# Dividing the opening feed-forward group of a streaming encoder layer like the two that follow it

## The chip, the cores and the metric

The kernel runs on one core of a Trainium2 chip. A core has a matrix engine (PE, whose weight loads are listed as PEld), a vector engine (DVE), a scalar engine (ACT), a small general engine (POOL) and a sequencer (SP) that issues nearly all transfers between the large memory (HBM) and the on-chip memory. Each engine works through its own list of instructions in order, and waits on semaphores for the others. The metric is the device time of one execution in microseconds (us), the median of several runs.

## The reference

One layer, with a prompt of 2048 tokens and 64 decode tokens, model width 1024, feed-forward width 2816. It is an attention-like half (a combined input projection, a pooling mixer and an mLSTM, an output projection) and a feed-forward half. The change touches the second half only in what it computes how, and the first in what is done beside it. The feed-forward half is:

```python
h2 = rmsnorm(x, g2) * (1 + sc2) + sh2
up = h2 @ w_up                                   # 1024 -> 2 x 2816
upp = jnp.concatenate([conv_buf.astype(up.dtype), up], 1)
conv = b_conv + sum(w_conv[j] * upp[:, j:j + T] for j in range(CONV_W))
a, g = jnp.split(conv, 2, -1)
x = x + gt2 * ((jax.nn.silu(g) * a) @ w_down)    # 2816 -> 1024
```

All of it is in 32-bit floating point.

## The kernel before, in words

**Numbers.** A 32-bit matrix is split by ACT into a rounded high part (line 411 for weights) and by DVE into the rest (line 414), and each product is three matmuls (high by high, high by low, low by high; `PASSES`). A weight unit is 128 x 512 of a matrix. SP loads it, ACT and DVE split it, and PE then uses it.

**The attention half** (0 to about 793 us) works through four groups of 512 tokens, the last with the 64 decode tokens added. In each group come the projections for v and the gates (line 1117), twelve projections for the four heads (line 477, with the mLSTM's small matmuls between them), four for the pooling mixer, and the eight rows of the output projection (line 477 too, from `mx`). In this half a scheduler orders the instructions of each engine.

**The feed-forward half** works through three groups of 704 tokens. In each group the 2816 features are 22 blocks of 128. The up projection of a block (line 1572) uses Strassen's scheme with seven products of 352 columns, 84 matmuls a block. Its weight sums (`wsum`) were worked out earlier, beside the attention half, by a generator called `up_sums`. In the list of weights each block has seven units; in the opening group all seven are split by ACT and DVE, and three of them are then stored in split form (`wsplit`, line 419), so that in the later groups only four are split and three are loaded ready.

The down projection comes after each part of the 22 blocks. `PARTS` says how they are divided. A plain part multiplies its blocks by 8 rows of output in two pieces of 448 and 256 columns (line 2138), 48 matmuls a block. A part of four blocks (`paired`) in the second and third group instead goes through `quad_down`, Strassen's scheme over two by two blocks of output rows, features and tokens (line 2015): 168 matmuls of 352 columns for four blocks. Its weight sums (`dsum`) come from `w_quad` and are worked out by the generator `quad_sums` in the opening group. For Strassen's scheme the gated activations are also added and subtracted on DVE before they are split (lines 1775, 1779, 1791).

**Order.** Here in the second half every engine but SP keeps the order in which the code is written. Generators of side work stand in lists `bg[0]` to `bg[4]`, and `tick(i)` runs the first of a list up to its next `yield`. `up_sums` stands in `bg[4]`, ticked four times in each projection of the attention half from the second group on, but not in the pooling projections, nor in the first two output rows. What is left of the lists is run at once in `leave`, after the first two output rows of the last group (`drain(1, 2, 3, 4)`). `leave` then closes the memory of the attention half and opens that of the feed-forward half (`f1`), and starts `norm_sums`, which loads the normed activations (`fscr` from `h2d`, line 802) and makes their sums and splits for the first up projection (`hx`, lines 764, 768 and 782). A side list `prepare` does the same for the next group while the current one runs.

Of the kernel before, what the change touches and what calls it, by code (L numbers as in the profile page):

```python
# [9 lines left out]
F32 = mybir.dt.float32  # L10
F32R = mybir.dt.float32r
AF = mybir.ActivationFunctionType
ALU = mybir.AluOpType
# [19 lines left out]
PARTS = (((0, 5), (5, 10), (10, 16), (16, 22)),) + (((0, 4), (4, 8), (8, 12), (12, 16), (16, 22)),) * 2  # L33
NQ = 4


def paired(g, part):
    return g > 0 and part[1] - part[0] == NQ
# [26 lines left out]
def tile_layer(ctx: ExitStack, tc: tile.TileContext, xT, vecs, cst, rst, w_mod, w_ada, w_qkou, w_v, w_pool,  # L65
# [276 lines left out]
    for g in range(NFG):  # L342
        held = None
        late = []
        for (f0, f1_) in PARTS[g]:
# [7 lines left out]
            if paired(g, (f0, f1_)):  # L353
                held = f0 // NQ
                continue
# [481 lines left out]
    if True:  # L837
# [6 lines left out]
        def up_sums():  # L844

            def load(f, c):
                w = a1.tile([P, 4, 256], F32, tag="w4", name="w4", bufs=4)
                for i in range(2):
# [3 lines left out]
            todo = [(f, c) for f in range(NF) for c in (0, 256)]  # L852
# [4 lines left out]
            for i, (f, c) in enumerate(todo):  # L857
                w = nx.pop(0)
                yield
# [12 lines left out]
                pin(nc.sync.dma_start(out=wsum[f, :, :, c:c + 256], in_=w))  # L872
# [748 lines left out]
    def quad_sums():  # L1621

        for d in range(8):
            for c in (0, 256):
                t = f2.tile([P, 2, FT], F32R, tag="av", name="qs", bufs=AVB)
                w = t.bitcast(F32).rearrange("p a t -> p (a t)")[:, :1024].rearrange("p (i c) -> p i c", i=4)
                nc.sync.dma_start(out=w, in_=w_quad[d, :, :, c:c + 256])
                for _ in range(5):
                    yield
                a11, a12, a21, a22 = (w[:, i] for i in range(4))  # L1630
                dve.tensor_tensor(out=a22, in0=a21, in1=a22, op=ALU.add)
                yield
                dve.tensor_tensor(out=a21, in0=a11, in1=a21, op=ALU.subtract)
                yield
                dve.tensor_tensor(out=a11, in0=a22, in1=a11, op=ALU.subtract)
                yield
                dve.tensor_tensor(out=a12, in0=a12, in1=a11, op=ALU.subtract)
                yield
                yield
                nc.sync.dma_start(out=dsum[d, :, :, c:c + 256], in_=w)  # L1640
                yield
                yield
                yield

# [647 lines left out]
```

## Time and profile before

| What | Value |
|---|---|
| Median of 3 runs | 2180.22 us (2180.21 to 2184.07) |
| Span of the profiled execution | 2178.0 us |
| PE, DVE, ACT busy | 2155.1, 1631.7, 1093.7 us |
| Opening feed-forward group, second, third | 468.2, 452.1, 464.2 us |
| Transfers | 539.51 MB, 248 GB/s over the span |

The groups' times are from the start of one group's first up projection to the next one's; the third ends with the span. A row of the timeline gives the start, the length, the engine, the line, the operands (out<-in) and how many instructions are merged. Lengths of matmuls overlap, so a pace is worked out from starts. In a table of windows each engine has its busy time and, in brackets, its instructions; the last two columns are the share of time that the 16 DMA engines were busy, and what they moved.

### The profile page before, as it was taken

The numbers are of one execution on the slowest core, as the hardware profiler recorded it, in microseconds if no ns is written. First come the engines' busy times: TensorE is split into PE (matmuls) and PEld (weight loads), VectorE is DVE, ScalarE is ACT, GpSimd is POOL, SyncE is SP. The second block draws the span as 40 slices with busy tenths as digits, with TensorE's granted clock in tenths as the row PEclk, the third lists the DMA queues.
The fourth block names the chain that finished last, engine by engine and source line by source line (L and its number), as shares of the span: only waits on it lengthen the run. The fifth ranks groups of instructions, "written<-read, shape, count | busy, mean of one in ns | idle before, by whom it ended". The sixth has DMA issues, their size and how long they took to land.

```text
span 2178.0 us, 38112 instructions
## 1 busy us (share of the span) xinstructions
PE 2155.1 (99%) x13553; PEld 2041.6 (94%) x13553; DVE 1631.7 (75%) x3040; ACT 1093.7 (50%) x2181; POOL 241.6 (11%) x474
## 2 busy tenths in 40 slices
PE   8999999999999999999999999999999999999998
PEld 7888888888899999999999999999999999999998
DVE  5868668757955678797967668888886587887874
ACT  4554335234333456474736445655655364565554
POOL 0010000001000101010101121100101331111112
PEclk9999999999999999999999999999999999999999
DMA  8886997988879387788967966666668675555542
GB/s 325 327 297 226 312 312 259 310 291 273 296 263 305 130 279 255 267 306 295 349 211 257 316 244 225 237 201 215 227 220 275 217 255 183 170 179 190 172 161 81
DMA packets 297351, 539.51 MB, mean 248 GB/s; under 512 B 25760, under 2 KB 114336, under 8 KB 297160
## 3 DMA queue, kind: packets, MB, share of 16 engines
q1 hardware_dynamic: 287720, 514.75, 69.8%
q10 hardware_dynamic: 9440, 22.32, 2.6%
q8 instruction: 107, 1.75, 0.3%
q14 instruction: 84, 0.69, 0.1%
HBM read 410.98 MB, written 125.98 MB: 247 GB/s over the span
## 4 chain that ended last, share of the span: by engine, by line
PE 82%; DMA 7%; DVE 7%; issue 2%; ACT 1%; SPq 1%; POOL 0%; DVEq 0%; POOLq 0%; ACTq 0%
PE mm L1572 35%; PE mm L477 19%; PE mm L2138 12%; PE mm L2015 8%; PE mm L1117 2%; DVE wt L414 2%; DMA raw<-w_ada 1%; DMA wt<-wsum 1%; DMA hl_kept<-wt 1%; DMA wsum<-w 1%; PE m L1307 1%; PE m L1329 1%; PE m L1327 1%; PE m L1292 1%; DVE scr L250 1%
## 5 line engine op out<-in xcount | busy, mean ns | idle before, releaser
L1572 PE MATMUL mm<-hx,wt 128*128 128x352 f32 x5544 | 887.0, 321 | 3.7 <-DVE hx L768 1.9
L1572 PEld LDWEIGHTS mm<-hx,wt 128*128 128x128 f32 x5544 | 878.6, 188 | 6.8 <-DVE hx L768 2.8
L477 PE MATMUL mm<-hl,wt 128*128 128x512 f32 (+2 forms) x1920 | 386.2, 357 | 0.2 <-ACT va L250 0.2
L411 ACT ACTIVATE wt<-raw 128x512 fp32r<-128x512 f32 (+3 forms) x470 | 276.8, 597 | 185.2 <-PE mm L477 63.5
L477 PEld LDWEIGHTS mm<-hl,wt 128*128 128x128 f32 x1920 | 315.4, 189 | 48.2 <-issue 5.3
L414 DVE TENSOR_TENSOR wt<-raw,wt 128x512 fp32r<-128x512 f32 (+3 forms) x470 | 312.2, 670 | 53.2 <-ACT wt L411 52.7
L2138 PE MATMUL mm<-av,wt 128*128 128x448 f32 (+1 forms) x1632 | 262.7, 322 | 0.0
L2138 PEld LDWEIGHTS mm<-av,wt 128*128 128x128 f32 x1632 | 250.4, 188 | 11.1
L1987 DVE SCALAR_TENSOR_TENSOR x<-mm,MOD,x 128x352 f32<-128x352 f32 (+3 forms) x360 | 167.2, 503 | 79.2 <-PE mm L2138 65.7
L2015 PE MATMUL mm<-av,wt 128*128 128x352 f32 x1344 | 220.6, 323 | 1.8 <-DVE x L1987 0.7
L2015 PEld LDWEIGHTS mm<-av,wt 128*128 128x128 f32 x1344 | 215.4, 188 | 4.8 <-DVE ea L1581 2.8
L1619 ACT ACTIVATE mm<-mm 128x352 f32<-128x352 f32 x196 | 87.8, 448 | 240.0 <-PE mm L1572 184.0
L477 PE MATMUL mm<-mx,wt 128*128 128x512 f32 (+1 forms) x960 | 182.6, 352 | 0.0
L477 PEld LDWEIGHTS mm<-mx,wt 128*128 128x128 f32 x960 | 159.3, 188 | 22.5
L1550 DVE SCALAR_TENSOR_TENSOR ta<-ea,V,ta 128x704 f32<-128x704 f32 (+1 forms) x132 | 125.6, 952 | 63.2 <-ACT ta L1545 51.2
L1550 DVE SCALAR_TENSOR_TENSOR tg<-eg,V,tg 128x704 f32<-128x704 f32 (+1 forms) x132 | 125.7, 952 | 61.0 <-ACT tg L1545 58.5
L414 DVE TENSOR_TENSOR wt<-wt 128x512 fp32r<-128x512 f32 x196 | 132.7, 683 | 12.8 <-ACT wt L411 12.7
L411 ACT ACTIVATE wt<-wt 128x512 fp32r<-128x512 f32 x196 | 119.2, 622 | 43.1 <-DMA wt<-wsum 40.1
L1759 ACT ACTIVATE tg<-tg 128x704 f32<-128x704 f32 (+1 forms) x66 | 52.5, 795 | 70.5 <-DVE tg L1550 70.5
L1528 POOL COPY ea<-UC 128x2 f32<-128x2 f32 x66 | 32.8, 497 | 482.6 <-DVE ta L1550 394.0
L1117 PE MATMUL mm<-wt,hl 128*128 128x256 f32 (+1 forms) x576 | 71.3, 284 | 0.0
L1117 PEld LDWEIGHTS mm<-wt,hl 128*128 128x128 f32 x576 | 70.4, 190 | 0.8 <-issue 0.6
(304 smaller groups left out, 2188.2 us busy)
## 6 DMA issues: line engine op xcount, KB each, us to landing
wt<-wsplit SPq DMA_DIRECT2D x132, 512.0 KB, 4.2
raw<-w_up SPq DMA_DIRECT2D x198, 256.0 KB, 3.8
wt<-hl_kept SPq DMA_DIRECT2D x96, 512.0 KB, 6.0
wt<-wsum SPq DMA_DIRECT2D x132, 256.0 KB, 5.3
wsplit<-wt SPq DMA_DIRECT2D x66, 512.0 KB, 5.5
w<-w_up SPq DMA_DIRECT2D x88, 256.0 KB, 3.7
wsum<-w SPq DMA_DIRECT2D x44, 512.0 KB, 4.9
Bd<-fscr ACTq DMA_DIRECT2D x56, 352.0 KB, 4.3
```

The costliest lines, as they stand in the source:

```text
L411: act.activation(u.w[:, 0, :u.n], u.raw[:, :u.n], AF.Copy)
L414: dve.tensor_tensor(out=u.w[:, 1, :u.n], in0=u.raw[:, :u.n], in1=u.w[:, 0, :u.n].bitcast(F32), op=ALU.subtract)
L477: pe.matmul(ps[bi][:, :hi - lo], U[:, a, k % 4 * P:(k % 4 + 1) * P], mv[k][:, b, lo:hi], start=(at == 0 and pi == 0), stop=(k == order[-1] ...
L1117: pe.matmul(ps[ti][:n, :cols], h[4 * kh + k4][:, b, lo:lo + n], U[:, a, k4 % 2 * cols:(k4 % 2 + 1) * cols], start=(kh == 0 and k4 == 0 and ...
L1528: pool.tensor_copy(ext[:, 0:2], UC[:, f, :])
L1550: dve.scalar_tensor_tensor(out=t[:, :E], in0=ext[:, j:j + E], scalar=wc(j, f), in1=t[:, :E], op0=ALU.mult, op1=ALU.add)
L1572: pe.matmul(bk.t[:, :FH], U[:, a, kc * P:(kc + 1) * P], Bo.at(nm, kc, b), start=(first and kc == 0 and pi == 0), stop=(kc == 3 and pi == 2 ...
L1619: act.activation(to.t[:, :FH], bk.t[:, :FH], AF.Copy)
L1759: act.activation(self.tg[:, :E], self.tg[:, :E], AF.Silu)
L1987: dve.scalar_tensor_tensor(out=x3[n][:, a:b], in0=bk.t[:, a - lo:b - lo], scalar=gt2(n, s), in1=x3[n][:, a:b], op0=ALU.mult, op1=ALU.add)
L2015: pe.matmul(bk.t[:, :FH], U[:, a, c:c + P], quad.put(op, m, b), start=(first and m == 0 and pi == 0), stop=(m == 1 and pi == 2), skip_grou ...
L2138: pe.matmul(bks[i].t[:, :hi - lo], U[:, a, k % 4 * P:(k % 4 + 1) * P], av[k][:, b, lo:hi], start=(k == 0 and (a, b) == PASSES[0]), stop=(k ...
```

## The change

All three groups use the same `PARTS`, and `paired` no longer asks for the group. So in the opening group sixteen of the 22 blocks go through `quad_down` in four parts of four, and the last six stay plain. The sums `dsum` are needed earlier: `quad_sums` goes, and its sixteen pieces are appended to the list of `up_sums`, behind the 44 pieces of `wsum`. A piece then takes three ticks where it took four.

```diff
-PARTS = (((0, 5), (5, 10), (10, 16), (16, 22)),) + (((0, 4), (4, 8), (8, 12), (12, 16), (16, 22)),) * 2
+PARTS = ((0, 4), (4, 8), (8, 12), (12, 16), (16, 22))
 NQ = 4
-def paired(g, part):
-    return g > 0 and part[1] - part[0] == NQ
+def paired(part):
+    return part[1] - part[0] == NQ
...
             def load(f, c):
                 w = a1.tile([P, 4, 256], F32, tag="w4", name="w4", bufs=4)
+                if f >= NF:
+                    tc.keep_in_program_order(nc.sync.dma_start(out=w, in_=w_quad[f - NF, :, :, c:c + 256]))
+                    return w
                 for i in range(2):
...
-            todo = [(f, c) for f in range(NF) for c in (0, 256)]
+            todo = [(f, c) for f in range(NF + 8) for c in (0, 256)]
...
             for i, (f, c) in enumerate(todo):
                 w = nx.pop(0)
-                yield
                 yield
...
-                pin(nc.sync.dma_start(out=wsum[f, :, :, c:c + 256], in_=w))
+                pin(nc.sync.dma_start(out=(wsum[f] if f < NF else dsum[f - NF])[:, :, c:c + 256], in_=w))
...
-    def quad_sums():
-        for d in range(8):
-            for c in (0, 256):
-                t = f2.tile([P, 2, FT], F32R, tag="av", name="qs", bufs=AVB)
-                w = t.bitcast(F32).rearrange("p a t -> p (a t)")[:, :1024].rearrange("p (i c) -> p i c", i=4)
-                nc.sync.dma_start(out=w, in_=w_quad[d, :, :, c:c + 256])
...
-        for pi, part in enumerate(PARTS[o.g]):
+        for pi, part in enumerate(PARTS):
...
-            quad = Quad() if paired(o.g, part) else None
+            quad = Quad() if paired(part) else None
...
-                    if o.g == 0:
-                        bg[0].append(quad_sums())
                     bg[1].append(prepare(fgroups[o.g + 1], fscr))
```

The line numbers of the changed file differ: 1574 there is 1572 before, 1993 is 2015, 2114 is 2138; 865, 866, 868 and 869 are 863, 864, 866 and 867, and 874 is 872.

**PE, opening feed-forward group.** Before, the first plain part comes behind the fifth block's products:

```order
L1572 MATMUL mm<-hx,wt 128x352 x330
L2138 MATMUL mm<-av,wt 128x448 x3
L2138 MATMUL mm<-av,wt 128x256 x3
...
L1572 MATMUL mm<-hx,wt 128x352 x12
L2138 MATMUL mm<-av,wt 128x448 x9
L2138 MATMUL mm<-av,wt 128x256 x9
```

and with the change:

```order
L1574 MATMUL mm<-hx,wt 128x352 x330
L719 MATMUL m_9599<-fscr,ones_r 128x352
L720 MATMUL m_9599<-fscr,ones_r 128x352
L719 MATMUL m_9603<-fscr,ones_r 128x352
L720 MATMUL m_9603<-fscr,ones_r 128x352
L1993 MATMUL mm<-av,wt 128x352 x24
L1574 MATMUL mm<-hx,wt 128x352 x12
L1993 MATMUL mm<-av,wt 128x352 x144
L1574 MATMUL mm<-hx,wt 128x352 x324
```

Four such passes of 168 stand where three plain parts of five, five and six blocks stood; PE's order ahead of this place is the same but for one matmul. In all 768 plain matmuls go and 672 of 352 columns come.

**DVE, first output rows of the last attention group** (`w` is the tile of a piece of sums, the rows of line 250 end an output row, line 768 is the first split of `norm_sums`). Before:

```order
L250 SCALAR_TENSOR_TENSOR scr<-mm,MOD,scr 128x64
L863 TENSOR_TENSOR w_7516<-w_7516 128x256
L414 TENSOR_TENSOR wt<-raw,wt 128x512
L864 TENSOR_TENSOR w_7516<-w_7516 128x256
L866 TENSOR_TENSOR w_7516<-w_7516 128x256
L867 TENSOR_TENSOR w_7516<-w_7516 128x256
L414 TENSOR_TENSOR wt<-raw,wt 128x512
L250 SCALAR_TENSOR_TENSOR scr<-mm,MOD,scr 128x256 x2
```

With the change:

```order
L250 SCALAR_TENSOR_TENSOR scr<-mm,MOD,scr 128x64
L865 TENSOR_TENSOR w_7627<-w_7627 128x256
L414 TENSOR_TENSOR wt<-raw,wt 128x512
...
L869 TENSOR_TENSOR w_7627<-w_7627 128x256
L865 TENSOR_TENSOR w_7687<-w_7687 128x256
...
L869 TENSOR_TENSOR w_7687<-w_7687 128x256
L865 TENSOR_TENSOR w_8264<-w_8264 128x256
L866 TENSOR_TENSOR w_8264<-w_8264 128x256
L250 SCALAR_TENSOR_TENSOR scr<-mm,MOD,scr 128x256 x2
L250 SCALAR_TENSOR_TENSOR scr<-mm,MOD,scr 128x64
L868 TENSOR_TENSOR w_8264<-w_8264 128x256
L414 TENSOR_TENSOR wt<-raw,wt 128x512
L869 TENSOR_TENSOR w_8264<-w_8264 128x256
```

Three pieces stand there in place of one, and the last of them ends behind the next output row's addition.

**SP, the same place.** Before:

```order
L640 DMA x2d<-scr 128x576
L872 DMA wsum<-w_7382 512x1x256
L872 DMA wsum<-w_7516 512x1x256
L594 DMA scr<-xT 128x576
L390 DMA raw<-wo_in 128x512
L390 DMA raw<-w_up 128x512
L802 DMA fscr<-h2d 128x704 x4
```

With the change:

```order
L874 DMA dsum<-w_7627 512x1x256
L390 DMA raw<-w_up 128x512
L874 DMA dsum<-w_7687 512x1x256
L640 DMA x2d<-scr 128x576
L390 DMA raw<-w_up 128x512
L874 DMA dsum<-w_8264 512x1x256
L594 DMA scr<-xT 128x576
L390 DMA raw<-w_up 128x512
L802 DMA fscr<-h2d 128x704 x4
```

The first load of `norm_sums` (line 802) stands behind the last store of a piece in both, and its memory is that of the pieces; there are three stores ahead of it now and there were two.

More of the change, by code (lines that the diff above doesn't have):

```diff
@@ L344, in tile_layer @@
         late = []
-        for (f0, f1_) in PARTS[g]:
+        for (f0, f1_) in PARTS:
             for f in range(f0, f1_):
@@ L352, in tile_layer @@
                     held, late = None, []
-            if paired(g, (f0, f1_)):
+            if paired((f0, f1_)):
                 held = f0 // NQ
```

18 lines of the change are left out of this document (1 added, 17 removed).

## The prediction

> **What bounds the kernel now.** I read the page's shares first, then its chain of waits by engine.
>
> ```profile
> span 2178.0 us, 38112 instructions
> PE 2155.1 (99%) x13553; PEld 2041.6 (94%) x13553; DVE 1631.7 (75%) x3040; ACT 1093.7 (50%) x2181; POOL 241.6 (11%) x474
> PE 82%; DMA 7%; DVE 7%; issue 2%; ACT 1%; SPq 1%; POOL 0%; DVEq 0%; POOLq 0%; ACTq 0%
> ```
>
> PE is busy in 99% of the span, so a matmul removed is worth its pace, as long as PE is fed. Then the table of windows, cut where the first up projection of the opening and of the next group starts, and PE's waits in the opening group (first three rows) and in the next (last two).
>
> ```profile
> 793.50:1261.70 468.20, 465.29 (x2922) 456.26 (x2921) 358.63 (x593) 258.17 (x468) 47.21 (x95) 1.00 0.81 278
> 1261.70:1713.80 452.10, 450.89 (x2831) 446.63 (x2830) 359.80 (x580) 256.25 (x473) 52.65 (x97) 1.00 0.68 232
> ...
> PE mm L1572 <- DVE hx L768: 1.9, 3, 0.8
> PE mm L1572 <- DVE wt L414: 0.8, 1, 0.8
> PE mm L1572 <- DVE eg L1581: 0.2, 1, 0.2
> ...
> PE mm L2015 <- DVE x L1987: 0.7, 1, 0.7
> PE mm L2015 <- DVE wt L414: 0.4, 1, 0.4
> ```
>
> The columns are PE, PEld, DVE, ACT, POOL, the granted clock, the DMA share and GB/s. The second group already does what the change makes of the opening one: it is 16.1 us shorter. Of this 2.9 - 1.1 = 1.8 us are waits, so 14.3 us is the work. This is the model for the sum, but the opening group has three things the second lacks: its start hangs on sums made just before, it splits seven weight units a block and not four, and its `dsum` must come from the attention half.
>
> **Term 1, the matmuls: -13.8 us.** The pace is read from starts in PE's timeline, the last plain part of the opening group first, then one Strassen pass of the second.
>
> ```profile
> 1213.92 4.04 PE L2138 MATMUL mm<-av,wt 128*128 128x448 f32 x24
> 1217.79 2.06 PE L1572 MATMUL mm<-hx,wt 128*128 128x352 f32 x12
> 1219.69 42.15 PE L2138 MATMUL mm<-av,wt 128*128 128x448 f32 x264
> 1261.68 0.64 PE L1572 MATMUL mm<-hx,wt 128*128 128x352 f32 x3
> ...
> 1409.41 4.19 PE L2015 MATMUL mm<-av,wt 128*128 128x352 f32 x24
> 1413.44 2.06 PE L1572 MATMUL mm<-hx,wt 128*128 128x352 f32 x12
> 1415.34 23.23 PE L2015 MATMUL mm<-av,wt 128*128 128x352 f32 x144
> 1438.41 51.65 PE L1572 MATMUL mm<-hx,wt 128*128 128x352 f32 x324
> ```
>
> Six plain blocks take (1217.79 - 1213.92) + (1261.68 - 1219.69) = 45.9 us for 288 matmuls, 0.159 us each. A pass takes (1413.44 - 1409.41) + (1438.41 - 1415.34) = 27.1 us for 168, 0.161 each. All 22 blocks plain are 1056 x 0.1592 = 168.1 us; four passes and six plain blocks are 4 x 27.1 + 45.9 = 154.3 us. The difference is 13.8 us, 0.5 below the 14.3 of the two groups.
>
> **Term 2, the start of the half: +4.0 us.** The chain of waits around 758 us, with DVE's and SP's timeline there, shows what the opening group's start hangs on.
>
> ```profile
> 758.43 5.40 DMA wsum<-w
> 763.91 3.18 DMA fscr<-h2d
> 802.08 7.24 PE mm L1572 x44
> ...
> 756.13 0.41 DVE L863 TENSOR_TENSOR w<-w 128x256 f32<-128x256 f32 x1
> 757.98 0.42 DVE L867 TENSOR_TENSOR w<-w 128x256 f32<-128x256 f32 x1
> 759.15 0.69 DVE L414 TENSOR_TENSOR wt<-raw,wt 128x512 fp32r<-128x512 f32 x1 [0.75 <-ACT wt L411]
> 761.54 1.07 DVE L250 SCALAR_TENSOR_TENSOR scr<-mm,MOD,scr 128x256 f32<-128x256 f32 x3 [1.70 <-PE mm L477]
> ```
>
> The last store of a piece goes out at 758.43, lands 5.4 us later, and only then may the first load of `norm_sums` go (763.91), since it overwrites the pieces' memory; from there the chain runs through `hx` to PE at 802, where PE loses the 1.9 us above. With the change three pieces stand where one stood. The first ends at 758.4 as now; the second's four instructions (0.42 each) with a split between them (about 0.6) end at 760.7; half of the third follows, then the output row's addition, which PE releases at 761.54, then the other half with a split: 764.0. The last store moves by 764.0 - 758.4 = 5.6 us, and so does the first load. About 1.7 us of DVE's other work there (one more addition of an output row and one of a sum of squares stand ahead of the first `hx` split in the new order) is done meanwhile and no longer in the way. I take 4.0; the bounds are 0, if the chain behind has slack that its rows do not show, and 5.6.
>
> **Term 3, DVE in the four passes: +2.2 us.** One pass with the blocks behind it is 80.4 us in the second group. The last two rows are DVE's densest stretches in the opening group now; below them is one block's splits back to back.
>
> ```profile
> 1329.00:1409.40 80.40, 80.34 (x505) 80.05 (x505) 69.20 (x116) 49.50 (x93) 6.48 (x16) 1.00 0.64 218
> ...
> 955.20:968.10 12.90, 12.90 (x83) 12.90 (x82) 12.79 (x23) 9.57 (x18) 1.66 (x4) 1.00 0.97 357
> 1060.50:1075.00 14.50, 13.74 (x85) 13.39 (x85) 13.49 (x23) 10.86 (x20) 1.55 (x4) 1.00 1.02 371
> ...
> 1070.20 1.28 DVE L414 TENSOR_TENSOR wt<-wt 128x512 fp32r<-128x512 f32 x2
> ```
>
> DVE has 69.2 us of work in 80.4 us. In the opening group three more units a block are split, 12 in such a stretch; two take 1.28 us, so 12 take 7.7 us, and DVE has 76.9 us, 96%. `quad_sums` is gone from there, which the 69.2 never held. The two dense rows say what 96% costs: at 12.79 of 12.90 us PE lost nothing, at 13.49 of 14.50 it lost 0.76, the one wait of 0.8 above. I take one such loss in each of the four stretches, 3.2 us, less the 1.0 us of waits on `L414` and `L1581` that go with the old parts: 2.2. The bounds are 0.1 (the 1.1 us of the second group) and 6.6: if DVE is never busier than 13.49 of 14.50 (93%), a stretch takes 76.9 / 0.93 = 82.7, 2.3 more, 9.2 in four, with a part of the 1.0 and of the last stretch, which holds less of `prepare`, off. ACT, at 49 of 80 us in the second group, is far from this.
>
> **Term 4, the pieces in the attention half: +1.5 us.** Sixteen pieces more are 64 DVE instructions and 32 transfers of 0.5 MB. They do not spread: a piece now takes three ticks, so the three projection stretches hold 16 pieces each and not 12.
>
> ```profile
> 236.00:340.00 104.00, 103.83 (x559) 86.15 (x559) 69.90 (x161) 35.27 (x106) 7.73 (x9) 1.00 0.91 302
> 410.00:514.00 104.00, 104.00 (x587) 87.38 (x580) 68.31 (x157) 35.59 (x101) 6.08 (x8) 1.00 0.88 290
> 600.00:706.00 106.00, 104.97 (x780) 99.41 (x780) 60.40 (x164) 40.65 (x126) 6.50 (x9) 1.00 0.86 284
> ...
> SPq L849 <- DMA wsum<-w: 97.1, 36, 5.9
> SPq L395 <- PE mm L477: 22.3, 22, 3.5
> SPq L395 <- PE mm L1117: 13.0, 8, 2.7
> ```
>
> DVE has room (70 of 104 us, and four pieces are 4 x 4 x 0.42 = 6.7 us). The transfers hardly have: the first stretch moves 31.4 MB at a share of 0.91, so 332 GB/s would be full; with 4 x 1.05 MB more it needs 35.6 / 332 = 107.2 us of its 104. The others come to 104.2 of 104 and 104 of 106. What hides this is the lead of the weight loads: SP waited 35.3 us for PE to free a buffer (the L395 rows), and at shares of 0.97 and 1.02 (the dense rows) PE lost no more than the 0.76 above. The bounds are 0 and the 3.4 us of overflow; I take 1.5, nearer to the dense rows. The Trainium skill, DMA: Bandwidth & Descriptors, Specifications, gives about 358 GB/s from HBM for a core, by which 35.6 MB would need 99.4 us (an estimate) and this term would be 0; in this trace the dense rows reach 371, so that figure is no firm limit here, and 332 is that stretch's own.
>
> **The sum** is made against the profiled execution: 2178.0 - 13.8 + 4.0 + 2.2 + 1.5 = 2171.9 us of span. The median of the runs is 2.2 us above this span, so 2174.1, and I predict 2174 us, 0.28% less. The work of `quad_sums` leaves the opening group for nothing: it stood on DVE and on the queue, not on PE.
>
> **The rivals.** (A) *SP is blocked by the pieces, and the change is slower.* In row L849 a load of a piece waits 36 times, 97.1 us in all, 2.7 each, for an earlier piece's store to land, and everything behind it on SP waits too, the attention half's weights above all. Sixteen pieces more, closer together, add 16 x 2.7 = 43 us. Against it speaks that the 97 us cost PE nothing, and the 35.3 us of SP's own lead. But that lead is spread over the half, and the waits fall into the projection stretches; if half of it counts there, 43 - 18 = 25 us come to PE: 2174.1 - 1.5 + 25 = 2198 us. It makes the change slower from 12 us on.
>
> (B) *DVE sets the pace of the passes*, at the upper bound of term 3: 2174.1 + 4.4 = 2178.5. For it speaks 96%, and that work waits in order behind additions that PE releases; against it, 12.79 of 12.90 without a loss.
>
> (C) *The losses are hidden*: terms 2 and 4 are near 0 and 3 near its lower bound: 2178.0 - 13.8 + 0.1 + 2.2 = 2166.5. For it speaks that the second group lost 1.1 us only; against it, that the store is on the chain of waits.
>
> **How the numbers follow.** The sum as worked out has a chance of 0.60, A 0.12, B 0.15, C 0.13. About 0.2% (4.4 us) is what a measurement of this kernel can tell from no change, so faster is below 2175.9 and slower above 2184.6. The forecast's own range, 2169 to 2179, from terms 2 to 4 partly at their bounds, lies with 0.46 below 2175.9, 0.13 within and 0.01 above. C is faster; B is 0.02 faster, 0.11 the same, 0.02 slower; A is 0.02 the same, 0.10 slower. In all: faster 0.61, the same 0.26, slower 0.13. From 2166 to 2183 the range holds C's time, the forecast and B; A is left out above and a little below.
>
> **What would show it.** Term 1: line 1993 with 2016 matmuls, and four passes of some 27 us in the opening group. Term 2: the first load of line 802 about 5 us later against the end of the attention half, and PE's wait for `hx` at 6 us and not 1.9. Term 3: PE's waits for DVE in the passes of the opening group near 3 us, with DVE over 90% there. Term 4: PE's waits and starts between 214 and 742 us as before, with the DMA share near 1 in the three stretches. The prediction is wrong if the attention half ends more than 5 us later (A), or if the stretches of the opening group are longer than 83 us (B).

## The result and the profile after

The changed kernel takes 2202.95 us (median of 4 runs, 2200.3 to 2205.5) against 2182.07 us for the kernel before in the same comparison: ratio 1.0096, 95% interval 1.0084 to 1.0109. It is 21 us slower, where 2174, 6 us below the 2180.22 of the kernel before, had been forecast; 2203 lies far outside 2166 to 2183. Times are medians of the executions in the fast state; one execution of the kernel with the pieces only, 2790 us at a granted clock of 0.713, is left out.

The page's span, its engines and the chain of waits by engine, after:

```profile
span 2203.7 us, 38114 instructions
...
PE 2152.6 (98%) x13457; PEld 2037.3 (92%) x13457; DVE 1685.8 (76%) x3152; ACT 1126.8 (51%) x2245; POOL 255.6 (12%) x474
...
PE 77%; DMA 9%; DVE 9%; issue 2%; ACT 2%; SPq 1%; POOL 0%; DVEq 0%; ACTq 0%; POOLq 0%
```

PE's busy time fell by only 2.5 us, its share of the chain from 82% to 77%; transfers and DVE took up what PE lost. The table of windows says in which stage (columns as in the prediction): the attention half from 214 us to the first up projection, the opening feed-forward group, the next group.

```profile
214.00:818.00 604.00, 584.50 (x3605) 517.06 (x3604) 428.67 (x955) 223.10 (x556) 39.58 (x58) 0.99 0.88 291
818.00:1288.60 470.60, 456.57 (x2826) 448.80 (x2825) 396.31 (x648) 292.70 (x536) 60.16 (x95) 0.99 0.76 256
1288.60:1740.50 451.90, 450.14 (x2824) 445.78 (x2823) 360.08 (x580) 256.68 (x472) 51.80 (x97) 1.00 0.69 232
```

The same stretch of the attention half was this before:

```profile
214.00:793.50 579.50, 578.31 (x3609) 514.75 (x3608) 412.97 (x897) 225.27 (x560) 38.13 (x58) 1.00 0.83 277
```

The first up projection starts at 818.0 and not 793.5: **24.5 us are lost in the attention half**, whose matmuls the change does not touch. PE is idle there for 604.0 - 584.5 = 19.5 us (1.2 before) and busy 6.2 us longer with the same work. The opening group takes 470.6 us; 468.2 before, 460.6 by the prediction's terms 1 to 3. The rest of the kernel is as long as it was (915.1 against 916.3 us from the second group on).

What PE, DVE and SP waited for between 214 and 818 us (total, times, longest, in us):

```profile
PE m L1309 <- DVE kw L250: 4.5, 4, 2.4
PE m L1331 <- DVE at L250: 3.0, 1, 3.0
PE m L1331 <- DVE SN L250: 2.6, 1, 2.6
PE m L1309 <- DVE at L250: 2.3, 1, 2.3
...
DVE w L865 <- DMA w<-w_quad: 20.8, 5, 6.6
DVE s L210 <- DMA raw<-w_ada: 20.1, 9, 4.6
DVE w L865 <- DMA w<-w_up: 18.8, 7, 3.9
...
SPq L852 <- DMA wsum<-w: 87.8, 38, 4.0
SPq L390 <- DVE wt L414: 29.9, 18, 3.9
SPq L849 <- DMA dsum<-w: 29.7, 11, 4.8
...
SPq L849 <- DMA wsum<-w: 13.5, 4, 3.9
```

No row has PE waiting for a weight. PE waits mostly for small steps of the mLSTM on DVE (`kw`, `at`, `SN`; 14.6 us, and 4.8 us for steps on ACT), and DVE, which works in order, waits 39.6 us for pieces (8.7 before) and 33.6 us in its two largest rows for `w_ada` (25.7 before). SP waits 131.0 us in 53 places for a piece's store to land; 97.1 in 36 before.

One such place, read through: SP's timeline, then DVE's, then PE's, after.

```profile
249.57 1.21 SPq L852 DMA_DIRECT2D w<-w_up  x2
250.88 0.56 SPq L874 DMA_DIRECT2D wsum<-w  x1
251.84 0.53 SPq L395 DMA_DIRECT2D wt<-hl_kept  x1
252.43 0.96 SPq L194 DMA_DIRECT2D raw<-w_ada  x1
256.31 1.22 SPq L852 DMA_DIRECT2D w<-w_up  x2
257.57 0.61 SPq L874 DMA_DIRECT2D wsum<-w  x1
...
253.01 0.74 DVE L210 SCALAR_TENSOR_TENSOR acc<-raw,CA,acc 128x512 f32<-128x512 f32 x1
...
258.23 0.75 DVE L210 SCALAR_TENSOR_TENSOR s<-raw,CA,s 128x512 f32<-128x512 f32 x1 [4.32 <-DMA raw<-w_ada]
...
260.31 0.68 DVE L250 TENSOR_TENSOR kw<-m,CL 128x512 f32<-128x512 f32 x1
...
261.14 1.13 PE L1309 MATMUL m<-va,kw 128*128 128x129 f32 x8 [1.44 <-DVE kw L250]
```

A store goes out at 250.88; the next piece's load overwrites the buffer of that store, so SP, two transfers later, stands still until 256.31, and the same again every 6 to 7 us. The load of `w_ada` of 252.43 is used at 258.23, DVE having waited 4.32 us for it, and `kw` comes behind that in DVE's order; PE waits 1.44 us for it.

A wait can cost PE more than its length. PE's timeline and four windows of 2 us around the wait of 2.40 us (the granted clock is the third number from the end):

```profile
285.22 1.16 PE L1309 MATMUL m<-va,kw 128*128 128x129 f32 x8 [2.40 <-DVE kw L250]
286.13 4.58 PE L477 MATMUL mm<-hl,wt 128*128 128x512 f32 x12
...
284.00:286.00 2.00, 0.78 (x7) 0.78 (x8) 1.90 (x4) 0.00 (x0) 0.00 (x0) 1.00 0.86 272
286.00:288.00 2.00, 2.00 (x9) 1.60 (x8) 1.92 (x5) 0.63 (x1) 0.00 (x0) 0.64 0.96 282
288.00:290.00 2.00, 2.00 (x6) 1.57 (x5) 2.00 (x6) 0.00 (x0) 0.00 (x0) 0.50 0.99 349
290.00:292.00 2.00, 2.00 (x16) 1.88 (x16) 0.76 (x3) 0.28 (x1) 0.00 (x0) 1.00 1.05 371
```

In the opening group, PE's largest waits, and three stretches from pass to pass:

```profile
PE mm L1574 <- DVE hx L768: 6.5, 2, 5.9
PE mm L1574 <- DVE wt L414: 3.8, 6, 1.0
PE mm L1993 <- DVE ea L1583: 1.9, 2, 0.9
...
894.40:977.30 82.90, 81.19 (x505) 80.00 (x505) 74.26 (x125) 54.38 (x102) 10.60 (x16) 1.00 0.72 244
977.30:1061.10 83.80, 81.82 (x506) 80.68 (x505) 76.45 (x128) 55.82 (x103) 10.72 (x17) 1.00 0.74 249
1061.10:1144.50 83.40, 81.19 (x506) 80.00 (x505) 74.03 (x124) 54.06 (x100) 7.42 (x16) 1.00 0.74 251
```

A stretch takes 83.4 us in the mean and not 80.4, with DVE at 75 of 83 us.

### The profile page after: what moved, and what is told of

Its sections match the earlier page's. It is cut to its first block, busy times and chain, and to the rows that moved or that the text cites. A ratio compares the mean times of both kernels' runs of the same rounds, so it can differ in the third digit from the quotient of the medians.

```text
span 2203.7 us, 38114 instructions
## 1 busy us (share of the span) xinstructions
PE 2152.6 (98%) x13457; PEld 2037.3 (92%) x13457; DVE 1685.8 (76%) x3152; ACT 1126.8 (51%) x2245; POOL 255.6 (12%) x474
## 4 chain that ended last, share of the span: by engine, by line
PE 77%; DMA 9%; DVE 9%; issue 2%; ACT 2%; SPq 1%; POOL 0%; DVEq 0%; ACTq 0%; POOLq 0%
PE mm L1574 35%; PE mm L477 17%; PE mm L1993 12%; PE mm L2114 6%; DMA raw<-w_ada 3%; DVE wt L414 2%; PE mm L1119 1%; DMA wsum<-w 1%; DMA dsum<-w 1%; DMA hl_kept<-wt 1%; DMA wt<-dsum 1%; DMA w<-w_quad 1%; DVE tg L1552 1%; DVE scr L250 1%; DVE s L210 1%
## 5 line engine op out<-in xcount | busy, mean ns | idle before, releaser
L477 PE MATMUL mm<-hl,wt 128*128 128x512 f32 (+2 forms) x1920 | 389.5, 359 | 1.1 <-ACT va L250 0.9
L477 PEld LDWEIGHTS mm<-hl,wt 128*128 128x128 f32 x1920 | 317.8, 190 | 50.1 <-issue 5.5
L414 DVE TENSOR_TENSOR wt<-raw,wt 128x512 fp32r<-128x512 f32 (+2 forms) x446 | 305.3, 690 | 52.0 <-ACT wt L411 51.8
L411 ACT ACTIVATE wt<-raw 128x512 fp32r<-128x512 f32 (+2 forms) x446 | 270.1, 611 | 143.8 <-PE mm L477 52.5
L1993 PE MATMUL mm<-av,wt 128*128 128x352 f32 x2016 | 330.9, 323 | 4.7 <-DVE ea L1583 2.4
L1993 PEld LDWEIGHTS mm<-av,wt 128*128 128x128 f32 x2016 | 323.0, 188 | 9.3 <-DVE ea L1583 5.5
L1621 ACT ACTIVATE mm<-mm 128x352 f32<-128x352 f32 x228 | 102.4, 449 | 264.2 <-PE mm L1574 180.2
L1965 DVE SCALAR_TENSOR_TENSOR x<-mm,MOD,x 128x352 f32<-128x352 f32 (+5 forms) x408 | 193.4, 513 | 56.5 <-PE mm L2114 39.2
L477 PE MATMUL mm<-mx,wt 128*128 128x512 f32 (+1 forms) x960 | 182.6, 352 | 0.0
L477 PEld LDWEIGHTS mm<-mx,wt 128*128 128x128 f32 x960 | 159.3, 188 | 22.5
L414 DVE TENSOR_TENSOR wt<-wt 128x512 fp32r<-128x512 f32 x228 | 154.5, 684 | 6.7 <-ACT wt L411 6.7
L411 ACT ACTIVATE wt<-wt 128x512 fp32r<-128x512 f32 x228 | 138.7, 622 | 32.8 <-DMA wt<-wsum 25.5
L2114 PE MATMUL mm<-av,wt 128*128 128x448 f32 (+1 forms) x864 | 139.0, 322 | 0.0
L2114 PEld LDWEIGHTS mm<-av,wt 128*128 128x128 f32 x864 | 132.5, 188 | 5.8
```

The lines of the kernel that those rows point to most:

```text
L411: act.activation(u.w[:, 0, :u.n], u.raw[:, :u.n], AF.Copy)
L414: dve.tensor_tensor(out=u.w[:, 1, :u.n], in0=u.raw[:, :u.n], in1=u.w[:, 0, :u.n].bitcast(F32), op=ALU.subtract)
L477: pe.matmul(ps[bi][:, :hi - lo], U[:, a, k % 4 * P:(k % 4 + 1) * P], mv[k][:, b, lo:hi], start=(at == 0 and pi == 0), stop=(k == order[-1] ...
L1621: act.activation(to.t[:, :FH], bk.t[:, :FH], AF.Copy)
L1965: dve.scalar_tensor_tensor(out=x3[n][:, a:b], in0=bk.t[:, a - lo:b - lo], scalar=gt2(n, s), in1=x3[n][:, a:b], op0=ALU.mult, op1=ALU.add)
L1993: pe.matmul(bk.t[:, :FH], U[:, a, c:c + P], quad.put(op, m, b), start=(first and m == 0 and pi == 0), stop=(m == 1 and pi == 2), skip_grou ...
```

## The experiments

Each time is a median beside runs of the kernel before on the same chip, the ratio with its 95% interval. "First up" is the start of the first up projection in the profiled execution (793.5 before, 818.0 with the change), the end of the attention half; it comes from one execution, so differences of 2 or 3 us there say little.

### Which part loses: the pieces without the passes, the passes without the pieces

```
pieces only:  PARTS as before (opening group in four plain parts); 60 pieces in up_sums
passes only:  PARTS as changed; for (f, c) over NF, not NF + 8, four ticks; dsum = wsum
```

> This kernel has the sixteen pieces in the attention half as the change has them, but the opening feed-forward group stays in four plain parts, so nothing reads `dsum` there. My theory: the loss is made in the attention half, 24.5 us up to the first up projection, and the late last store costs about 4.6 us more at `hx`; nothing is won. Expected 2182 + 24.5 + 4.6 = 2211 us, with the first up projection at about 818 us. Rival: the loss comes from DVE in the passes of the opening group and the attention half's delay is given back; then this kernel, which has no such passes, is near 2182 us.

Measured: 2201.18 against 2181.19 us, 1.0095 (1.0079 to 1.0112); first up 815.5. From there to the first pass of the second group 539.0 us, 535.5 before.

> This kernel has the opening group's four Strassen passes and no extra pieces in the attention half (44 pieces, four ticks each, as before). The weight sums are left out: where `dsum` was read, as many bytes of `wsum` are read, so the results of the second half are wrong and the work after the attention half is that of the change. My theory: attention half as before (first up projection at 793.5 us), opening group 13.8 us less for the matmuls and 6 us more for waits on DVE: 2182 - 7.8 = 2174 us. Rival (the passes themselves cost what they save, because DVE is at 96% there): 2182 us or more.

Measured: 2178.76 us, 0.9988 (0.9979 to 0.9998); first up 795.0.

Nearly the whole loss is there without a single pass, and the passes, free of their sums, win 2.4 us, not 13.8. Two things had thus gone wrong and not one. Of 2211 for the first I missed 10 us, of 2174 for the second 5.

### The opening group: DVE's splits

```
passes only, and:
-        return (kept, 512, WHOLE, None) if g else (wsum[f, :, i], 512, INSIDE, kept)
+        return (hl_kept[(3 * f + KEPT.index(i)) % 32, :, :, :512], 512, WHOLE, None)
```

> The kernel with the four passes and no extra pieces (2178.8 us), and in addition no splitting of the three kept units of a block: their halves are read whole in all groups (from other data of the same size, so the second half's results are wrong), and 66 splits on DVE (0.64 us each, 42 us) and on ACT and 66 stores leave the opening group. Theory B (DVE, at 96% there, sets the pace of the passes; 83.4 us a stretch against 80.4): the opening group comes to the second group's 452 us plus about 2 for its start, so 2178.8 - 11 = 2168 us. Rival (the stretches are longer for some other reason, such as the start of the half or the transfers): 2176 us or more.

Measured: 2169.71 against 2183.14 us, 0.9933 (0.9914 to 0.9952). Two stretches of the run with the passes only, then two of this one:

```profile
948.60:1031.90 83.30, 81.31 (x507) 80.12 (x506) 75.66 (x127) 55.35 (x103) 10.78 (x17) 1.00 0.74 248
1031.90:1114.90 83.00, 81.17 (x505) 80.01 (x505) 75.79 (x127) 55.57 (x103) 10.77 (x16) 1.00 0.73 255
```

```profile
865.20:945.70 80.50, 80.44 (x507) 80.15 (x506) 69.07 (x114) 49.14 (x91) 6.61 (x16) 1.00 0.65 217
945.70:1026.10 80.40, 80.35 (x506) 80.05 (x505) 68.79 (x114) 48.50 (x89) 6.34 (x16) 1.00 0.66 219
```

With 69 us of DVE work a stretch is the second group's 80.4; with 75.7 it is 83. The three kept splits a block cost 13.43 - 2.43 = 11.0 us of the 13.8 (a difference of two medians, good to some 4 us); the three stretches from pass to pass took 250.4 us in all with the passes only and 241.9 here, 8.5 less. ACT's half of the splits, the stores and the bytes left with them, so that it is DVE's half is argued only from its shares (91% of a stretch, and the `L414` row of PE's waits). In the two stretches above with the passes only DVE stood idle for 14.9 us, 10.6 of them waiting for ACT's `ta` and `tg` (in the second group 7.2 of 11.2 us of one stretch, at no loss), so ACT's half is a rival that no run separates. Giving DVE's half to POOL:

```
-            dve.tensor_tensor(out=u.w[:, 1, :u.n], ...
+            (pool if u.keep is not None and u.at >= n_att else dve).tensor_tensor(...
```

> The kernel with the four passes and no extra pieces (2178.8 us), the 66 kept splits' second instruction (a subtraction of 128x512) given to POOL instead of DVE. Theory B: DVE drops from 96% to about 87% in the passes; POOL has room (a 128x704 sum takes it 1.5 us, so 66 take some 75 us of 468), and the opening group gains up to the 11 us of the passes' excess: 2168 to 2172 us. Rival: POOL works in order behind copies that wait for DVE and ACT, so the units come late and PE waits for POOL instead: 2178 us or more.

Measured: 2192.34 us, 1.0037 (1.0024 to 1.0049): the rival's time and worse, but not by its path, for no row has PE waiting for POOL. The grouped rows of this run between 793 and 1290 us (POOL) and 864 and 1130 us (DVE), then the DVE row with the passes only:

```profile
L414 POOL TENSOR_TENSOR wt<-wt 128x512 fp32r<-128x512 f32 x65 | 98.1, 1511 | 242.1 <-ACT wt L411 222.7 <-PE mm L1575 17.8 <-DMA wt<-wsum 1.5
L1553 DVE SCALAR_TENSOR_TENSOR ta<-ea,V,ta 128x704 f32<-128x704 f32 x25 | 30.2, 1207 | 14.9 <-ACT ta L1548 14.4
```

```profile
L1553 DVE SCALAR_TENSOR_TENSOR ta<-ea,V,ta 128x704 f32<-128x704 f32 x24 | 22.8, 949 | 11.7 <-ACT ta L1548 11.2
```

A split takes POOL 1.51 us, and DVE's own instructions become longer (949 to 1207 ns in the mean for the same one). In the opening group of this run the 27 of these that overlap a split on POOL take 1430 ns in the mean, the 17 others 950. So DVE is not relieved: it is busy for 74 to 79 us of a stretch of 86 to 88.

### The attention half: sums, lead, or a part of the bytes

```
no piece sums:  the four dve.tensor_tensor of up_sums only if f < NF
two ahead:      range(3) -> range(2), i + 3 -> i + 2
short pieces:   the pieces with f >= NF carry columns c:c + 32, not c:c + 256
```

> The change with its sixteen pieces loaded and stored, but without their four DVE instructions each (`dsum` then holds `w_quad` as it is, so the results of the second half are wrong). My theory (transfers and SP's blocking waits are the cause; DVE is late because it waits for loads): nearly all of the loss stays, 2198 to 2203 us. Rival (DVE's own work of 64 x 0.42 = 27 us delays the mLSTM chain): about 2180 us.

Measured: 2201.57 us, 1.0095 (1.008 to 1.011); first up 817.9. The sums of the sixteen pieces are not the cause.

> The change with a piece loaded two pieces ahead and not three, all else equal: the buffer that a load overwrites was then stored one whole piece earlier, so SP need not wait for a store that was issued just before. Theory S (SP's waits for a store to land hold up everything behind them): SP's waits on `wsum` and `dsum` fall from 131 us to below 40 and the attention half's loss from 24.5 us to below 8: at most 2187 us. Theory D (the queue is full: 35.6 MB at 332 GB/s are 107 us of 104): the waits move elsewhere and the time stays at 2200 us within 4.

Measured: 2195.93 us, 1.0059 (1.004 to 1.0079); first up 814.5. SP's waits for stores to land fell to 35.5 us as both theories had it, but its waits at a store for DVE's sums (`L874 <- DVE w`) rose from 28 to 72 us, and other loads stand behind these too. DVE's waits for pieces stayed (41.5 us, 39.6 with the change). Neither theory; this edit trades one wait of SP for another.

> The change, but the sixteen pieces carry 32 of their 256 columns (an eighth of the bytes, in loads, sums and stores; `dsum` is not read, `wsum` is in its place, so the second half's results are wrong). As many transfers, waits and instructions stand on each queue as in the change. Theory S (SP is held up by the waits of loads for stores): the waits stay nearly as long (a store's landing is mostly fixed time), so at least two thirds of the 22 us stay: 2196 us or more. Theory D (the transfers' bytes fill the queue): 14.7 MB of the 16.8 MB more are gone, so at most 2187 us.

Measured: 2193.61 us, 1.0044 (1.003 to 1.0057); first up 814.4. Again between the two. The late start was better (PE has no wait for `hx` in the opening group), the attention half hardly. But the sixteen pieces stand last in the list, so the projection stretch from 236 us held as many bytes as with the change; the run could not speak of it.

### The pace and the place

```
three ticks alone:      passes only, with one yield less a piece
four ticks, pooling:    the change with one yield more a piece, and
-            if at in ups and not quiet:
+            if at in ups:
                 tick(4)
```

> The kernel with the four passes and no extra pieces (2178.8 us; first up projection at 795.0 us), but its 44 pieces take three ticks each, as in the change. So far the attention half lost 21 to 24 us with the sixteen pieces' sums left out, with an eighth of their bytes, and with other waits on SP; all these kernels have three ticks. Theory P (the denser pace shortens a load's lead from three pieces of four ticks to three of three, and the loads, held up on SP, come late for DVE): the loss is there without any extra piece in the two first groups, first up projection 10 us or more later than 795, 2189 us or more. Theory N (the number of pieces, so their waits over the whole half): at most 3 us later, 2179 to 2182 us.

Measured: 2187.06 against 2181.94 us, 1.0022 (1.0012 to 1.0031); first up 809.4, 14.4 us later with no piece more than before. As theory P has it in the attention half; the time, 2 us short of its bound. SP's waits for landings were 83.5 us here, less than the 97.1 before, so it is not their total that makes the loss.

> The whole change, but with four ticks a piece as before, and ticks for the pieces also in the pooling projections (where they rest in both kernels, and where the transfers' share is 0.75 to 0.83), so that 60 pieces fit at the old pace. Theory P: the attention half ends within 8 us of before, and the time is about 2184 to 2189 us (the passes' gain of 2.4 us less the late start of 4 to 7 us). Theory N: the loss of 21 to 24 us stays, 2198 us or more.

Measured: 2199.34 us, 1.008 (1.0065 to 1.0095); first up 816.1. Theory N's number: the old pace does not help once the pieces fill the pooling too. So both the pace (14.4 us alone) and the number of pieces count; that it comes down to how much stands in the queue, wherever it stands, is a guess that no run shows.

### Another queue

```
pieces on POOL:   quad_pieces(): 32 pieces of 128 columns, pool.dma_start and pool.tensor_tensor
own queue:        every nc.sync.dma_start of up_sums -> pool.dma_start; POOL's small steps -> dve
control:          only POOL's small steps -> dve
```

> The whole computation of the change, but the sums for `dsum` are made on POOL, in 32 pieces of 128 columns with a buffer of their own, loaded and stored on POOL's queue; DVE and SP hold the 44 pieces of before at four ticks each. As many bytes move as in the change. Theory S: SP and DVE are rid of the extra pieces, so the attention half ends within 6 us of before (793.5 us) and the time is that of the passes alone, 2179 to 2184 us. Theory D (bytes): the stretches stay overfull and most of the loss stays, 2195 us or more. A third way: POOL's sums or its waits delay the mLSTM's small POOL steps (`sf`), and PE waits for these.

Measured: 2245.01 us, 1.0285 (1.026 to 1.031); first up 859.7: the third way. DVE waited 63.6 us for the mLSTM's `sf` on POOL (13.0 with the change), which stood behind POOL's waits for its own transfers.

> The change with the transfers of all 60 pieces issued on POOL's queue and none on SP's; DVE makes the sums at three ticks as in the change. So that nothing of the attention half stands behind these transfers, POOL's own small steps in that half (copies, memsets, and the powers that make reciprocal square roots) are given to DVE, the powers as a multiplication and addition of constants, so the results are wrong. Theory S (SP held up by the pieces' waits makes the other loads on SP late): SP's waits on `wsum` and `dsum` (131 us) are gone from its queue, `w_ada` is on time and the attention half's loss of 24.5 us falls below 6. Theory V (DVE works in order and the pieces on it, with the waits for their own loads, are what delays the mLSTM chain): most of the loss, 15 us or more, stays. To be read against the control of this call.

Measured: 2355.02 against 2179.8 us, 1.0802 (1.0786 to 1.0818); first up 969.0. Two rows of DVE's waits:

```profile
DVE w L865 <- DMA w<-w_up: 142.1, 25, 18.2
DVE w L865 <- DMA w<-w_quad: 58.7, 6, 20.2
```

POOL issued the pieces so late that DVE waited 201 us for them, and the attention half lost 175. SP had nothing of the pieces in its queue here and waited 305 us for PE to free buffers (`L477`), and it helped nothing. So this run did not test SP; in it, late pieces on DVE cost nearly their whole lateness on PE.

> The control: the change with POOL's small steps of the attention half on DVE as in the run before it in this call, but the pieces' transfers on SP's queue as in the change. Both theories: within 4 us of the change (2203 us), its attention half ending at 814 to 820 us; if it is far below, the POOL steps were part of the loss.

Measured: 2193.07 us, 1.006 (1.0044 to 1.0077); first up 806.8, outside the 4 us I allowed. Perhaps the mLSTM chain has some slack back without the step on POOL inside it; I had no theory for that, and it was not followed up.

### Mending SP's order

```
-                if i + 3 < len(todo): nx.append(load(*todo[i + 3]))
-                pin(store of piece i)
+                if i + 2 < len(todo): nx.append(load(*todo[i + 2]))
+                pin(store of piece i - 1)
pooling too: and the tick without "not quiet"
```

> The whole change at its own pace (60 pieces, three ticks), but with the queue's order mended: a piece is loaded two pieces ahead, and its store is issued one piece later, behind the next piece's sums. So a load overwrites a buffer whose store was issued a whole piece before, and a store's sums are long done: neither should wait on SP. Theory S (a load that waits 5 us for the store just before it, and a store that waits for DVE, hold SP; `w_ada` and later pieces come late; DVE waits for them in order and the mLSTM chain with it): SP's waits on pieces fall from 131 + 23 us to below 40, DVE's on `w_ada` and pieces to those of before (34 us), the first up projection comes below 800 us (818 in the change), and the time is 2179 to 2186 us. Theory V (sixteen pieces more on DVE and in the transfers cost this much in any order): 2194 us or more.

Measured: 2195.54 against 2183.77 us, 1.0049 (1.0035 to 1.0062); first up 811.5. The waits for landings stayed at 74.2 + 25.6 + 10.7 = 110.5 us: with the load and the store both moved by one piece, the load at `i + 2` again overwrites the buffer whose store is the last one ahead of it on SP, exactly as in the change. The edit did not remove its cause, so it told nothing of it.

> The run before with ticks for the pieces also in the pooling projections, at three ticks: the last store then goes out some 60 us before the attention half ends and the start of the feed-forward half no longer waits for it. Theory S: 4 to 6 us less than the run before, 2176 to 2181 us, the passes' gain of 2.4 us with nothing to pay. If pieces in the pooling cost by themselves, as four ticks with pooling suggested (losses at 340 to 400 and 600 us): 2185 us or more.

Measured: 2230.96 us, 1.0218 (1.02 to 1.0236); first up 856.9. PE waited 29.2 us, up to 15.7 at once, for ACT's copies of weights; ACT itself waited up to 10.3 us for one load of `w_out`. The start of the half did come sooner (67.3 us from first up to first pass, 76.4 with the change), but at that price.

### Bytes against waits

```
all short:           all 60 pieces 32 of 256 columns wide, in loads, sums and stores
full, short sums:    full transfers, sums over 32 columns
no landing waits:    in_=w of the store -> in_=fixed (a tile that is never rewritten)
```

> The change with all 60 pieces cut to 32 of 256 columns, in loads, sums and stores (`wsum` and `dsum` are not read, kept weights of the same size are read in their place, so the second half's results are wrong). SP issues as many transfers with the same waits; their bytes fall from 63 to 8 MB, and DVE's sums from some 100 us to about 30 in all. The run with only the sixteen last pieces cut said little of the first stretches, where the 44 stand. Theory S (waits of loads for stores on SP, whose landing takes most of its time whatever the size): at least 12 of the 24.5 us of the attention half stay, first up projection at 807 us or later. Theory D (the denser pace fills the transfer engines: share 0.97 to 1.00 in the projection stretches, and every load lands late): first up projection at 793 to 799 us, time about 2179 to 2183 us.

Measured: 2173.47 against 2182.68 us, 0.9954 (0.9938 to 0.9971); first up 795.2. The time is 6 us below theory D's; from first up to the end this run took 1376.1 us, the one with the passes only 1382.0, and that is not explained (three ticks alone, with the same second half as the latter, took 1377.1, so a single execution can differ by as much).

> The companion: all 60 pieces with their full loads and stores, but sums over 32 columns only (same substitute reads, the second half's results are wrong). Theories S and D: the loss stays, first up projection at 812 us or later, because only DVE's time is less. Theory V (DVE's own time on the pieces): first up projection below 800 us. If this run and the one with short transfers both come out below 800 us, bytes and sums act only together.

Measured: 2192.35 us, 1.0041 (1.0026 to 1.0056); first up 812.4.

> The change with its pieces, sums, pace, lead and bytes unchanged, but every piece's store sends a fixed tile instead of the piece just summed (so `wsum` and `dsum` hold wrong values and the second half's results are wrong). A load then overwrites a buffer that no store reads, and SP waits neither for a store's landing (131 us in the change) nor, at a store, for DVE. Theory S (these waits on SP make the loads behind them late): the attention half's loss of 24.5 us falls below 8, first up projection before 801 us. Theory D (bytes: engines full in the projection stretches make every load land late): first up projection at 810 us or later.

Measured: 2189.05 against 2182.6 us, 1.0024 (1.001 to 1.0038), its runs from 2179.5 to 2194.0; first up 805.4. Windows of the run with short transfers, then of the one without landing waits, then of the change:

```profile
214.00:795.20 581.20, 578.14 (x3608) 514.60 (x3607) 383.18 (x964) 226.15 (x561) 36.42 (x58) 1.00 0.70 210
```

```profile
214.00:805.40 591.40, 581.63 (x3604) 514.87 (x3604) 432.11 (x959) 224.50 (x559) 39.63 (x58) 1.00 0.87 298
...
236.00:342.00 106.00, 106.00 (x566) 88.04 (x566) 76.47 (x179) 36.51 (x108) 8.19 (x11) 1.00 0.93 327
```

```profile
236.00:342.00 106.00, 102.16 (x539) 84.17 (x538) 72.29 (x172) 33.85 (x103) 8.15 (x9) 0.98 0.94 314
```

Both theories hold a part. With the store's source fixed, SP waits neither for a piece's store to land nor, at a store, for DVE (131.0 and 28 us in the change). At the same bytes 818.0 - 805.4 = 12.6 us of the 24.5 are gone, and the first projection stretch loses nothing although it moves more (327 GB/s, not 314): there these waits were the whole loss. The other 11.9 us stand in later stretches. The runs with short transfers and with short sums differ in the transfers alone, and 812.4 - 795.2 = 17.2 us of the attention half go with these; the sums alone are worth 818.0 - 812.4 = 5.6 us.

What the bytes do to other loads is seen in their landing (median us in the last column, between 236 and 700 us): before, with the change, without landing waits, all short.

```profile
raw<-w_ada SPq DMA_DIRECT2D x39, 256.0 KB, 4.7
```

```profile
raw<-w_ada SPq DMA_DIRECT2D x39, 256.0 KB, 5.3
```

```profile
raw<-w_ada SPq DMA_DIRECT2D x40, 256.0 KB, 5.7
```

```profile
raw<-w_ada SPq DMA_DIRECT2D x38, 256.0 KB, 4.0
```

Short transfers also shorten SP's waits for landings (67.3 us in all; a store of 64 KB landed in 2.6 us in the median, one of 512 KB in 4.9), so how the second half of the loss divides between late landings and what is left of the waits stays open.

The totals of the waits do not rank these kernels. DVE waited 57.5 us for pieces and `w_ada` with short transfers, at a loss of 1.7 us, and 42.5 without landing waits, at 11.9; 38.1 before. So a total gives no price; I take it that what stands behind a wait at that moment decides. The path from SP over DVE to PE is read in the place shown above; that it carries the whole loss is not shown.

No kernel that computes the whole layer was faster than the one before; the best that could be hoped for, the passes with their sums for nothing, is 2.4 us below it.

## Why the prediction was wrong

**Term 1, -13.8 us, was right.** `L1993` has 2016 matmuls; its first pass in the opening group takes (898.26 - 894.37) + (923.21 - 900.16) = 26.9 us, 27.1 forecast. Where DVE had room (no kept splits) the kernel gained 13.4 us, though that run also leaves out splitting, stores and bytes.

**Term 2, +4.0, was right.** The first load of line 802 went out 24.6 us ahead of the first up projection, 29.6 before, so 5.0 us later (5 forecast). PE's wait for `hx` went to 6.5 us (6 forecast, 1.9 before); with the pieces only, first up to the second group's first pass grew by 3.5 us.

**Term 3, +2.2, is the first step that failed**, in size and, as far as shown, not in mechanism: it measures 11.0 (8.5 in the three stretches alone), outside its own bounds of 0.1 to 6.6. The demand was right (76.9 us of DVE a stretch forecast, 74 to 76.5 measured). The price was read from two dense rows of 13 and 14.5 us, in which DVE could run at 93 to 99%. Over a stretch of 80 us it comes to 91% at most (75.8 of 83.0); most of its idle time there is spent waiting for ACT, and that this is never caught up is my reading of it. Rival B named this and the stretches of 83 us, but priced it at 2.3 us a stretch from the same 93%; they measure 3. It is not all of it either: in the run with the passes only PE's busy time in the opening group is 6.1 us longer than in the second group besides its idle time, with the clock at 1.00. The starts of the matmuls account for about 4 us of that: a matmul is listed with 0.32 us where the next starts after 0.16, so the first 0.16 us of each of 15 waits count as busy (2.5 us; 0.3 in the second group), and single matmuls, the first behind a wait among them, stand 0.27 us ahead of the next (3.5 us; 1.9). The rest is open.

**Term 4, +1.5, is the step that decided**: 24.5 measured, bounds 0 to 3.4. It counted DVE's time, rightly as nothing (the kernel without the sixteen sums is as slow), and the bytes against a full queue, 3.4 us at most. It then let "the lead of the weight loads" hide both. That lead held: PE waited for no weight. Nor did the share of the transfer engines come near 1: in the three stretches it was 0.94, 0.93 and 0.85 (0.91, 0.88 and 0.86 before). But the transfers have a second reader. DVE takes `w_ada` and the pieces in program order, with the mLSTM's steps behind them, and has no lead like PE's. The view of waits of the kernel before has them (8.7 us on pieces, 25.7 on `w_ada`); only PE's and SP's were priced. The order on SP, each load of a piece directly behind the store whose buffer it overwrites, stood in the kernel before as well. What the runs showed in the term's place: three ticks alone cost 14.4 us, the waits at SP for the pieces' stores 12.6 of the 24.5, and short transfers, at equally short sums, 17.2; how these overlap is open.

**Rival A** had the sign, the place and nearly the amount: SP's waits for stores 97 to 131 us (140 forecast), 25 us on PE (24.5), 2198 (2203). Its path was wrong: not the weights came late but `w_ada` and the pieces, and only about half of the loss goes with SP's waits at the pieces' stores. That its 25 us meet the 24.5 is therefore in part luck: they were 43 us of added waits, of which 34 came, less half of SP's lead. Its chance of 0.12 rested on the sentence that the 97 us "cost PE nothing" before. That was true, and the sentence is no price: with three ticks alone SP waited less for landings (83.5 us), and PE lost 14.4.

The sum by what was measured: -13.8 + 3.5 + 11.0 + 24.5 = 25.2; the spans differ by 25.7. That it closes so well is luck too, with 11.0 good to some 4 us.

## What to carry to other kernels

Before work is moved into a stage that "has room", list everything that reads the queue it will use, and for each reader what stands behind it in order; a lead for the matmul's weights says nothing about loads that a vector engine takes in order inside a recurrence. A load that overwrites a buffer whose store was just issued holds its whole queue until the store has landed, here 2.5 us in the mean and up to 4.8: before, 97 us of such waits cost PE nothing, and with the change 131 us of them were worth half of the loss at most. Such a total is therefore no price; look at what stands behind each wait. An engine's ceiling is read over a stretch as long as the one to be forecast: DVE ran at 99% for 13 us and at 91% for 83.

## What was not expected of the hardware

The granted clock of PE fell to 0.50 for some 3.4 us after waits of 2.40 and 2.61 us, and for longer during the wait of 5.9 us for `hx`: 12 matmuls of 128x512 took 4.58 us after the first, and after the last 22 matmuls took 5.04 us, 0.229 each and not 0.16. But the length of a wait does not decide alone, for one of 3.04 us, the longest between 214 and 818 us, left the clock at 1.00:

```profile
455.36 0.49 PE L1331 MATMUL m<-va,at 128*128 128x129 f32 x2 [3.04 <-DVE at L250]
...
456.00:458.00 2.00, 2.00 (x14) 1.77 (x14) 1.15 (x4) 0.73 (x3) 0.00 (x0) 1.00 0.85 291
```

Between its first wait for input and its last microseconds the kernel before had no wait longer than 1.3 us, and its clock stood at 1.00 there. Summed over windows of 2 us, the clock withheld 3.4 us in the attention half of the changed kernel. The Trainium skill, TensorE: Matmul & The Clock Gate, Part 1: The HAM clock gate, says that the clock halves after an idle window of about 3.4 us in a free-running count. The half rate agrees with the 0.50 here, and so does the 3.4 us; the waits of 2.40 and 2.61 us that were enough are shorter than that window, and there the measurement decides.

DVE slows down while POOL computes: the same 128x704 instruction took 949 ns and, with 66 splits on POOL, 1207 ns in the mean. The Trainium skill, GPSIMD Engine Reference, 1. Specifications, lists the on-chip memory interfaces as shared with VectorE, with contention for DVE instructions of two inputs. This row agrees: instructions that take one input from a product (`x<-mm,MOD,x`) stayed at 576 and 581 ns. Transfers issued on POOL came so late that DVE waited up to 20.2 us for one.
